# Gate and up projections of a SwiGLU layer as 2x2x2 block products with seven multiplications

## The chip, the cores and the metric

The kernel runs on one core of one Trainium2 chip. The metric is the device time of one execution in microseconds (us). The engines are named as in the profile: PE (TensorE, matmul), PEld (its weight loads), DVE (VectorE), ACT (ScalarE), POOL (GpSimd) and SP (SyncE, which here issues DMAs).

## The reference

One layer of a decoder, 512 tokens of 1024 channels, in float32: a mixer (stick-breaking attention and a gated convolution), a cross-attention to 256 memory tokens, and the feed-forward sublayer that the change is about, which ends in a final norm. Each has its own RMS norm and residual addition.

```python
hf = rms_norm(x, norm_ffn[l])
gate, up = jnp.split(hf @ w_ffn_in[l], 2, axis=-1)      # 1024 -> 2 x 2816
x = x + (jax.nn.silu(gate) * up) @ w_ffn_out[l]         # 2816 -> 1024
...
return rms_norm(x, norm_final)
```

## The kernel before

Activations lie transposed, features on the 128 partitions and the 512 tokens along the free axis. A matrix product is a loop over k tiles of 128 input features, and every product of two float32 values is made of three float32r matmuls: each operand is split into a high part (a cast on ACT, line 149 for weights, line 168 or 171 for activations) and a low part (a subtraction on DVE, line 150, 169 or 172), and `mm3` (lines 154 to 156) adds high x high, high x low and low x high into one PSUM bank.

`load_w` (line 138) loads 128 x 1024 weights over SP's queue into a `wr` buffer and splits them into `wh` and `wl`; each of the three has four buffers. `gemm` (line 158) runs eight k tiles, 24 matmuls of 512 columns, into one bank. The activations' parts come from `upool`, 50 buffers of 128 x 512, and float32 temporaries from `tpool`, seven.

`residual` (line 481) computes x + w.T @ act for eight feature tiles m, keeps the new x, splits x times the next norm's gain into two parts, and adds up the squares. The norm's factor 1/rms is not in these parts: it is applied to the results of the next product. `squares_mean` (line 176) gives it, along the tokens, by two matmuls of the squares' sum (`acch`, `accl`) into `varb` (line 196) and a short chain on ACT and DVE (lines 124 to 130); for this sublayer it is called `r2b`.

The gate and up projections (lines 578 to 593) loop over the 22 hidden tiles m of 128. For each, a `gemm` of the gate columns goes to tile `fg`, one of the up columns to `fu`; DVE scales both by `r2b` (lines 585 and 591), ACT applies Silu to the gate (line 586), DVE multiplies them (line 592), and the product is split into two parts. The matmuls for the token means stand between the first gate and the first up product.

Then the output projection runs over the hidden tiles k: each is 24 matmuls, three for each of eight output tiles, which occupy all eight PSUM banks. The last four k tiles are kept back (`HOLD`), and `finish` (line 613) runs them for one half of the tokens and then the other, 256 columns at a time: for each m it adds the residual (line 621), squares it on ACT (line 625) and adds up the squares on DVE (line 627). `store` (line 636) multiplies by the final norm's factor, on POOL for the first half and on DVE and POOL for the second (line 641), and writes the output.

The order on each engine is set at compile time by a scheduler that goes by the program's order and by what is ready; waits for data and for free buffers follow from the tiles.

Of the kernel before, what the change touches and what calls it, by code (L numbers as in the profile page):

```python
# [8 lines left out]
F32 = mybir.dt.float32  # L9
F32R = mybir.dt.float32r  # L10
# [14 lines left out]
HID = 2816  # L25
NF = HID // P
EPS = 1e-6
HOLD = 4                # FFN-out k tiles kept back, so that the last sum can finish by token half
MEM_AT = (1, 3, 5, 7)   # attention steps that square the memory's tiles
MEAN_AT = 9             # and the step that takes their mean, between two pairs of heads  # L30
EARLY = 2               # merge tiles whose gate projections run beside the attention
FIRST = 4               # weight loads that queue behind the stream's

# [4 lines left out]
def hybrid_layer(ctx: ExitStack, tc: tile.TileContext, xT_d, memT_d, cols_d, wv_d, win_d,  # L38
# [40 lines left out]

# [1 line left out]
    ident = cpool.tile([P, P], F32, tag="ident", name="ident")  # L81
# [29 lines left out]
    def log_exp_tables(last):  # L111
        """Has the table set that holds both Ln and Exp loaded behind an instruction."""
        i = nc.scalar.preload_act_table_set("natural_log_exp_and_others")
        after(i, [last])
        return [i]

    def rstd_of(var, n, s, tables=()):
        """1 / sqrt(var + eps) for [P, n] mean squares, refined by one Newton step."""
        def new(t):
            return tmp(t, n) if n > TT else spool.tile([P, n], F32, tag=t, name=nm(t))  # L120

        v, y, a = new("rv"), new("ry"), new("ra")
        r = cpool.tile([P, n], F32, tag=s, name=nm(s))
        after(nc.scalar.activation(y, var, AF.Ln, bias=eps_t), tables)
        nc.vector.tensor_scalar(out=v, in0=var, scalar1=EPS, scalar2=None, op0=ALU.add)  # L125
        exps.append(nc.scalar.activation(y, y, AF.Exp, scale=-0.5))
        nc.vector.tensor_tensor(out=a, in0=y, in1=y, op=ALU.mult)
        nc.vector.scalar_tensor_tensor(out=a, in0=a, scalar=-0.5, in1=v, op0=ALU.mult,
                                       op1=ALU.mult)
        nc.vector.scalar_tensor_tensor(out=r, in0=a, scalar=1.5, in1=y, op0=ALU.add, op1=ALU.mult)  # L130
        return r

    def chained(i):
        """Keeps the first loads in their order of issue."""
        after(i, chain[-1:])
        chain.append(i)

    def load_w(src, cols=P):
        """Loads [P, 1024] of weights and splits them into two float32r parts."""
        k = D // cols  # L140
        raw = wpool.tile([P, D], F32, tag="wr", name=nm("wr"))
        i = nc.sync.dma_start(raw, src)
        if count[1] < FIRST:
            count[1] += 1
            chained(i)
        hi = wpool.tile([P, k, cols], F32R, tag="wh", name=nm("wh"))
        lo = wpool.tile([P, k, cols], F32R, tag="wl", name=nm("wl"))
        h2, l2 = (t.rearrange("p k c -> p (k c)") for t in (hi, lo))
        nc.scalar.copy(h2, raw)  # L149
        nc.vector.tensor_tensor(out=l2, in0=raw, in1=f(h2), op=ALU.subtract)  # L150
        return hi, lo
# [6 lines left out]
    def gemm(ps, w, act, k0=0):  # L158
        """ps[feature, token] = sum over k of w[k].T @ act[k]."""
        n = len(act)  # L160
        for k in range(n):
            mm3(ps, (w[0][:, k0 + k, :], w[1][:, k0 + k, :]), act[k], k == 0, k == n - 1)

    def split(src, s, scale=None, cols=512):
        """src (* scale) as two float32r parts; src may lie in PSUM."""
        hi, lo = unit(s + "h", cols), unit(s + "l", cols)
        if scale is None:
            nc.scalar.copy(hi, src)
            nc.vector.tensor_tensor(out=lo, in0=src, in1=f(hi), op=ALU.subtract)
        else:  # L170
            nc.scalar.activation(hi, src, AF.Copy, scale=scale)
            nc.vector.scalar_tensor_tensor(out=lo, in0=src, scalar=scale, in1=f(hi),
                                           op0=ALU.mult, op1=ALU.subtract)
        return hi, lo

    def squares_mean(acc, n):
        """acc: the squares' sum over feature tiles, for n tiles of tokens."""
        parts = unit("acch", n * P), unit("accl", n * P)
# [3 lines left out]
        def by_token(s, tables=()):  # L182
            """1 / rms with tokens on partitions, [P, n]."""
            vp = otile("var")
# [7 lines left out]
        def along(s, tables=()):  # L192
            """1 / rms with tokens along the free axis, on all partitions."""
            vp = otile("varb")[:, :n * P]
# [5 lines left out]

# [1 line left out]
    xg, wv = [], []  # L202
# [16 lines left out]

# [1 line left out]
    vps = [ztile("v") for _ in range(TT)]  # L221
# [6 lines left out]

# [1 line left out]
    def project(col):  # L230
# [49 lines left out]

    # ---- stick-breaking attention, z^T by key tile and two heads; the weights that follow a key
    # tile's own are summed on the tensor engine, in the bank that holds z ----
    oT = []
# [91 lines left out]
    def mem_square(k2):  # L375
        """The squares' sum of two feature tiles of the memory."""
        mk = f(unit("mk")).rearrange("p (j t) -> p j t", j=2)
# [36 lines left out]
    stick.close()  # L414
    xpool = ctx.enter_context(tc.tile_pool(name="xpool", bufs=12))

# [1 line left out]
    mg = []  # L418
# [12 lines left out]

# [1 line left out]
    merged = []  # L433
# [18 lines left out]

# [1 line left out]
    km = []  # L454
# [25 lines left out]

    def residual(w_dram, act, old, gain):
        """x^T = old + w.T @ act; x^T, x^T * gain in two parts, and the squares' mean of x."""
        xs, xn = [], []
        acc = tmp("acc")
        for m in range(KD):
            w = load_w(w_dram[m])
            ps = mmtile("r")
            gemm(ps, w, act)
            xm = xpool.tile([P, S], F32, tag="x", name=nm("x"))
            if old is None:  # L490
                nc.sync.dma_start(xm, xT_d[m * P:(m + 1) * P, :])
            nc.vector.tensor_tensor(out=xm, in0=ps, in1=xm if old is None else old[m], op=ALU.add)
            xs.append(xm)
            xn.append(split(xm, "xg", gain[:, m:m + 1]))
            if m == 0:
# [8 lines left out]

# [1 line left out]
    om = []  # L506
# [66 lines left out]

    x2T, x2g, mean2 = residual(wmo_d, om, x1, g_ffn)

# [1 line left out]
    act = []  # L577
    for m in range(NF):
        w = load_w(wfi_d[m])
        ps = mmtile("fg")  # L580
        gemm(ps, w, x2g)
        if m == 0:
            r2b = mean2[1]("r0b")
        g = tmp("fg")
        nc.vector.tensor_tensor(out=g, in0=ps, in1=r2b, op=ALU.mult)  # L585
        silu = nc.scalar.activation(g, g, AF.Silu)
        w = load_w(wfi_d[NF + m])
        ps = mmtile("fu")
        gemm(ps, w, x2g)
        u = tmp("fu")  # L590
        nc.vector.tensor_tensor(out=u, in0=ps, in1=r2b, op=ALU.mult)  # L591
        nc.vector.tensor_tensor(out=u, in0=u, in1=g, op=ALU.mult)
        act.append(split(u, "act"))

# [1 line left out]
    acc = [mmtile("f") for _ in range(2)] + [ztile("f") for _ in range(4)]  # L596
    acc = acc[2:] + [otile("f") for _ in range(2)] + acc[:2]

    def out_step(m, k, w, sl):
        fs = slice(m * P, (m + 1) * P)  # L600
        mm3(acc[m][:, sl], (w[0][:, 0, fs], w[1][:, 0, fs]), (act[k][0][:, sl], act[k][1][:, sl]),
            k == 0, k == NF - 1, skip_group_check=True)

    for k in range(NF - HOLD):
        w = load_w(wfo_d[k], D)
        for m in range(KD):
            out_step(m, k, w, slice(0, S))
    held = [load_w(wfo_d[k], D) for k in range(NF - HOLD, NF)]
    tables = log_exp_tables(silu)
    hs = S // 2  # L610
    yg = {}

    def finish(half):
# [3 lines left out]
        for m in range(KD):  # L617
            for i, w in enumerate(held):
                out_step(m, NF - HOLD + i, w, sl)
            y = x2T[m][:, sl]  # L620
            nc.vector.tensor_tensor(out=y, in0=acc[m][:, sl], in1=y, op=ALU.add)
            if m == 0:
# [33 lines left out]
def _layout(x, mem, norm_mix, w_in, conv_w, w_branch_a, w_branch_b, w_mix_out, norm_mem_q,  # L656
# [3 lines left out]
    def by_column(w, cols=P, k=KD):  # L660
        """[K, N] -> [N / cols, P, K / P, cols], flat in each partition."""
        n = w.shape[1] // cols
        return w.reshape(k, P, n, cols).transpose(2, 1, 0, 3).reshape(n, P, k * cols)

    def by_row(w):
        """[1024, 512] -> [4, P, 2 * 512]."""
        return w.reshape(4, 2, P, 512).transpose(0, 2, 1, 3).reshape(4, P, 1024)

    gains = np.stack([norm_mix[0], norm_mem_q[0], norm_mem_kv[0], norm_ffn[0], norm_final])
# [14 lines left out]
        "w_mem_o": by_column(w_mem_o[0]),  # L684
        "w_ffn_in": by_column(w_ffn_in[0]),
        "w_ffn_out": w_ffn_out[0].reshape(NF, P, D),
# [19 lines left out]
```

## Time and profile before

| What | Value |
|---|---|
| Median of 3 runs | 900.91 us (899.91 to 901.19) |
| The profiled execution: span from first to last instruction | 901.2 us |
| PE busy, share of the span | 883.5 us, 98% |
| PEld busy | 735.6 us, 82% |
| DVE busy | 497.7 us, 55% |
| ACT busy | 370.4 us, 41% |
| POOL busy | 40.0 us, 4% |

The profile is of one execution; its span is that execution's time, 0.3 us above the median of the runs. A line such as "L155 PE MATMUL fu<-xgl,wh 128*128 128x512 f32 x176 | 68.5, 389 | 0.0" is a group of instructions: program line, engine, operation, output and inputs, shapes, count, then busy us, mean ns of one, and idle us of the engine before them. In a timeline, the two numbers ahead are start and length in us. Matmuls are pipelined, so their recorded lengths overlap.

### The profile page before, as it was taken

How to read it: one execution, taken by the hardware profiler on the slowest of the kernel's cores; microseconds unless marked ns; L12 is line 12 of the kernel's file. 1: busy time of each engine (PE TensorE's matmuls, PEld its weight loads, DVE VectorE, ACT ScalarE, POOL GpSimd, SP SyncE). 2: the span in 40 equal slices, each digit the busy share in tenths (PEclk: the TensorE clock that was granted, in tenths of full speed). 3: DMA queues.
4: the chain of work that ended last, by engine and by line, in shares of the span. 5: the costliest groups of instructions: out<-in, count | busy, mean ns of one | idle time of the engine just before them, and what ended most of it. 6: DMA issues, size and time to landing. Idle time of an engine off the chain costs nothing.

```text
span 901.2 us, 10745 instructions
## 1 busy us (share of the span) xinstructions
PE 883.5 (98%) x4210; PEld 735.6 (82%) x4210; DVE 497.7 (55%) x751; ACT 370.4 (41%) x607; POOL 40.0 (4%) x89
## 2 busy tenths in 40 slices
PE   7999999999999999999999999999999999999995
PEld 5878887888888898888888888888888888888894
DVE  5768787886544566555546564444444434322236
ACT  6566565565332344433434442222332223221133
POOL 0021221111000000000000000000000000000003
PEclk9999999999999999999999999999999999999998
DMA  7332212226222245432121222233222233222202
GB/s 280 117 106 82 82 60 70 71 71 211 94 94 93 94 140 188 145 111 96 48 71 46 95 94 94 96 100 107 95 94 94 94 97 109 98 94 93 71 1 94
DMA packets 29490, 89.85 MB, mean 100 GB/s; under 512 B 3056, under 2 KB 7168, under 8 KB 29440
## 3 DMA queue, kind: packets, MB, share of 16 engines
q1 hardware_dynamic: 28864, 88.62, 28.9%
q8 instruction: 33, 0.54, 0.3%
q10 hardware_dynamic: 544, 0.52, 0.2%
q14 instruction: 17, 0.14, 0.1%
q0 software_dynamic: 32, 0.03, 0.0%
HBM read 87.06 MB, written 2.10 MB: 99 GB/s over the span
## 4 chain that ended last, share of the span: by engine, by line
PE 96%; DVE 2%; ACT 1%; DMA 0%; issue 0%; DVEq 0%; POOL 0%; POOLq 0%; ACTq 0%
PE pr L154 7%; PE pr L155 7%; PE pr L156 7%; PE fu L155 4%; PE fg L155 4%; PE fg L156 4%; PE fu L156 4%; PE fu L154 4%; PE fg L154 4%; PE f L154 4%; PE f L155 4%; PE f L156 4%; PE r L154 3%; PE r L155 3%; PE r L156 3%; PE mq L154 2%
## 5 line engine op out<-in xcount | busy, mean ns | idle before, releaser
L149 ACT CAST wh<-wr 128x1024 fp32r<-128x1024 f32 x150 | 157.6, 1052 | 424.0 <-issue 175.6
L150 DVE TENSOR_TENSOR wl<-wr,wh 128x1024 fp32r<-128x1024 f32 x150 | 183.5, 1223 | 121.2 <-ACT wh L149 120.9
L154 PE MATMUL pr<-xgh,wh 128*128 128x512 f32 x288 | 113.0, 392 | 0.1
L156 PE MATMUL pr<-xgh,wl 128*128 128x512 f32 x288 | 112.5, 391 | 0.0
L155 PE MATMUL pr<-xgl,wh 128*128 128x512 f32 x288 | 112.5, 390 | 0.0
L154 PE MATMUL f<-acth,wh 128*128 128x512 f32 (+1 forms) x208 | 74.4, 358 | 0.0
L155 PE MATMUL f<-actl,wh 128*128 128x512 f32 (+1 forms) x208 | 74.0, 356 | 0.0
L156 PE MATMUL f<-acth,wl 128*128 128x512 f32 (+1 forms) x208 | 74.0, 357 | 0.0
L155 PE MATMUL fu<-xgl,wh 128*128 128x512 f32 x176 | 68.5, 389 | 0.0
L154 PE MATMUL fu<-xgh,wh 128*128 128x512 f32 x176 | 68.5, 389 | 0.0
L154 PE MATMUL fg<-xgh,wh 128*128 128x512 f32 x176 | 68.5, 389 | 0.0
L156 PE MATMUL fg<-xgh,wl 128*128 128x512 f32 x176 | 68.5, 389 | 0.0
L155 PE MATMUL fg<-xgl,wh 128*128 128x512 f32 x176 | 68.5, 389 | 0.0
L156 PE MATMUL fu<-xgh,wl 128*128 128x512 f32 x176 | 68.5, 389 | 0.0
L154 PEld LDWEIGHTS pr<-xgh,wh 128*128 128x128 f32 x288 | 54.4, 189 | 11.5 <-issue 0.4
L156 PEld LDWEIGHTS pr<-xgh,wl 128*128 128x128 f32 x288 | 54.2, 188 | 11.4
L155 PEld LDWEIGHTS pr<-xgl,wh 128*128 128x128 f32 x288 | 54.3, 188 | 10.8
L591 DVE TENSOR_TENSOR fu<-fu,r0b 128x512 f32<-128x512 f32 x22 | 15.2, 691 | 66.8 <-PE fu L156 66.8
L154 PEld LDWEIGHTS f<-acth,wh 128*128 128x128 f32 x208 | 39.3, 189 | 6.0 <-DVE rv L125 0.2
L155 PEld LDWEIGHTS f<-actl,wh 128*128 128x128 f32 x208 | 39.3, 189 | 5.6
L156 PEld LDWEIGHTS f<-acth,wl 128*128 128x128 f32 x208 | 39.1, 189 | 5.7
L585 DVE TENSOR_TENSOR fg<-fg,r0b 128x512 f32<-128x512 f32 x22 | 15.2, 692 | 49.0 <-PE fg L156 48.9
(216 smaller groups left out, 1655.2 us busy)
## 6 DMA issues: line engine op xcount, KB each, us to landing
wr<-in_w_ffn_in_dram SPq DMA_DIRECT2D x44, 512.0 KB, 3.2
wr<-in_w_in_dram SPq DMA_DIRECT2D x36, 512.0 KB, 3.3
wr<-in_w_ffn_out_dram SPq DMA_DIRECT2D x22, 512.0 KB, 3.2
wr<-in_w_branch_dram SPq DMA_DIRECT2D x8, 512.0 KB, 3.2
wr<-in_w_mem_k_dram SPq DMA_DIRECT2D x8, 512.0 KB, 3.3
wr<-in_w_mem_v_dram SPq DMA_DIRECT2D x8, 512.0 KB, 3.9
wr<-in_w_mix_out_dram SPq DMA_DIRECT2D x8, 512.0 KB, 3.3
wr<-in_w_mem_q_dram SPq DMA_DIRECT2D x8, 512.0 KB, 3.2
```

The costliest lines, as they stand in the source:

```text
L149: nc.scalar.copy(h2, raw)
L150: nc.vector.tensor_tensor(out=l2, in0=raw, in1=f(h2), op=ALU.subtract)
L154: nc.tensor.matmul(ps, a[0], b[0], start=start, stop=False, **kw)
L155: nc.tensor.matmul(ps, a[0], b[1], start=False, stop=False, **kw)
L156: nc.tensor.matmul(ps, a[1], b[0], start=False, stop=stop, **kw)
L585: nc.vector.tensor_tensor(out=g, in0=ps, in1=r2b, op=ALU.mult)
L591: nc.vector.tensor_tensor(out=u, in0=ps, in1=r2b, op=ALU.mult)
```

## The change

The 1024 input features are taken as four pairs of k tiles, the tokens as two halves of 256, and a hidden tile's gate and up columns as the two output rows: a 2x2 block matrix of weights times a 2x2 block matrix of activations. Seven products of blocks (Strassen's scheme in Winograd's form) take the place of eight. For each hidden tile m:

- `ffn_weights` loads gate and up weights (two loads of 128 x 1024, in a new layout in which the two k tiles of each pair are apart) and forms four sums of 128 x 512: s1, s2 and s4 on POOL, each from the one before, and s3 on DVE. The two gate blocks are split in one piece of 1024 columns, the other five operands (s1, s2, s3, s4 and one up block) in pieces of 512.
- `product` runs one block product: four pairs x three split terms, 12 matmuls of 256 columns.
- `ffn_pair` strings the seven products together. Some add to a bank that holds an earlier product; ACT copies the sum so far out of PSUM first (c1, u2, u3), and DVE adds what belongs together. PE's order is written out: the products 4, 5, 6 of tile m alternate with 1, 2, 3 of tile m + 1, then comes 7 of tile m. The token means' matmuls stand behind the first three products.
- Only the gate is scaled by `r2b`; the up side's factor is applied behind the output projection, in `finish`, by a multiplication out of PSUM ahead of the residual's addition.
- The residual before this stage makes, for each pair of feature tiles, the seven activation forms (`forms_of`: four additions on DVE, seven casts on ACT, seven subtractions on DVE, all 256 wide). They hold 28 of the 50 `upool` buffers, the unsplit activations 22; the activations are split behind the loop.
- `x` is updated in place, with `xpool` at 8 buffers for 12, and comments are taken out.

```diff
+    def forms_of(xe, xo):
+        b12, b22 = xe[:, HS:], xo[:, HS:]
+        c = tmp("c1")
+        n1, t3 = c[:, :HS], c[:, HS:]
+        nc.vector.tensor_tensor(out=n1, in0=xe[:, :HS], in1=b12, op=ALU.subtract)
+        nc.vector.tensor_tensor(out=t3, in0=b22, in1=b12, op=ALU.subtract)
+        c = tmp("c2")
+        n2, t4 = c[:, :HS], c[:, HS:]
+        nc.vector.scalar_tensor_tensor(out=n2, in0=n1, scalar=-1.0, in1=b22, op0=ALU.mult,
+                                       op1=ALU.subtract)
+        nc.vector.scalar_tensor_tensor(out=t4, in0=n2, scalar=-1.0, in1=xo[:, :HS], op0=ALU.mult,
+                                       op1=ALU.subtract)
+        made = []
+        for raw in (xe[:, :HS], xo[:, :HS], n1, n2, t3, t4, b22):
+            u = unit("xf")
+            nc.scalar.copy(u[:, :HS], raw)
+            nc.vector.tensor_tensor(out=u[:, HS:], in0=raw, in1=f(u[:, :HS]), op=ALU.subtract)
+            made.append(u)
+        return made
...
-            xn.append(split(xm, "xg", gain[:, m:m + 1]))
+            if pairs:
+                raw = tmp("xr")
+                nc.scalar.activation(raw, xm, AF.Copy, scale=gain[:, m:m + 1])
+                if m % 2:
+                    xn.append(forms_of(even, raw))
+                else:
+                    even = raw
+            else:
+                xn.append(split(xm, "xg", gain[:, m:m + 1]))
...
-    for m in range(NF):
-        w = load_w(wfi_d[m])
-        ps = mmtile("fg")
-        gemm(ps, w, x2g)
-        if m == 0:
-            r2b = mean2[1]("r0b")
+    KP = KD // 2
+    def parts(raw, pool, tag):
+        w = pool.tile([P, 2, 512], F32R, tag=tag, name=nm("wf"))
+        nc.scalar.copy(w[:, 0, :], raw)
+        nc.vector.tensor_tensor(out=w[:, 1, :], in0=raw, in1=f(w[:, 0, :]), op=ALU.subtract)
+        return w[:, 0, :], w[:, 1, :]
+    def ffn_weights(m):
+        wg = wpool.tile([P, D], F32, tag="wr", name=nm("wr"))
+        nc.sync.dma_start(wg, wfi_d[m][:, :D])
+        wu = wpool.tile([P, D], F32, tag="wr", name=nm("wr"))
+        nc.sync.dma_start(wu, wfi_d[m][:, D:])
+        a21, a22 = wu[:, :512], wu[:, 512:]
+        s1 = fpool.tile([P, 512], F32, tag="w2", name=nm("s1"), bufs=4)
+        nc.gpsimd.tensor_tensor(out=s1, in0=a21, in1=a22, op=ALU.add)
+        s3 = fpool.tile([P, 512], F32, tag="w2", name=nm("s3"), bufs=4)
+        nc.vector.tensor_tensor(out=s3, in0=wg[:, :512], in1=a21, op=ALU.add)
+        hi = wpool.tile([P, D], F32R, tag="wh", name=nm("wh"))
+        lo = wpool.tile([P, D], F32R, tag="wl", name=nm("wl"))
+        nc.scalar.copy(hi, wg)
+        nc.vector.tensor_tensor(out=lo, in0=wg, in1=f(hi), op=ALU.subtract)
+        a11, a12 = wg[:, :512], wg[:, 512:]
+        s2 = fpool.tile([P, 512], F32, tag="w2", name=nm("s2"), bufs=4)
+        nc.gpsimd.tensor_tensor(out=s2, in0=s1, in1=a11, op=ALU.add)
+        s4 = fpool.tile([P, 512], F32, tag="w2", name=nm("s4"), bufs=4)
+        nc.gpsimd.tensor_tensor(out=s4, in0=s2, in1=a12, op=ALU.add)
+        return [(hi[:, :512], lo[:, :512]), (hi[:, 512:], lo[:, 512:]), parts(s1, wpool, "wh"),
+                parts(s2, wpool, "wl"), parts(s3, wpool, "wh"), parts(a22, wpool, "wl"),
+                parts(s4, fpool, "wf")]
+    def product(ps, w, i, first, last):
+        ps = ps[:, :HS]
+        for k in range(KP):
+            hi, lo = (x[:, k * P:(k + 1) * P] for x in w[i])
+            x = x2f[k][i]
+            for j, (a, b) in enumerate(((lo, x[:, :HS]), (hi, x[:, :HS]), (hi, x[:, HS:]))):
+                nc.tensor.matmul(ps, a, b, start=first and k == 0 and j == 0,
+                                 stop=k == KP - 1 and j == 2, skip_group_check=True)
+    def ffn_pair(m):
+        w = ffn_weights(m)
+        z, v, y = ztile("z"), ztile("v"), otile("y")
+        sa, sb = tmp("sa"), tmp("sb")
+        c1, u2, u3, c22 = sa[:, :HS], sa[:, HS:], sb[:, :HS], sb[:, HS:]
         g = tmp("fg")
...
+        product(z, w, 0, True, True)
+        nc.scalar.copy(c1, z[:, :HS])
+        yield
+        product(v, w, 1, True, True)
+        nc.vector.tensor_tensor(out=g[:, :HS], in0=v[:, :HS], in1=c1, op=ALU.add)
+        yield
+        product(y, w, 2, True, True)
+        yield
+        product(z, w, 3, False, True)
+        nc.scalar.copy(u2, z[:, :HS])
+        yield
+        product(z, w, 4, False, True)
+        nc.scalar.copy(u3, z[:, :HS])
+        nc.vector.tensor_tensor(out=c22, in0=y[:, :HS], in1=u3, op=ALU.add)
+        yield
+        product(z, w, 5, False, True)
+        yield
+        product(y, w, 6, False, True)
+        nc.vector.tensor_tensor(out=g[:, HS:], in0=y[:, :HS], in1=u2, op=ALU.add)
+        nc.vector.tensor_tensor(out=g, in0=g, in1=r2b[0], op=ALU.mult)
+        silu[0] = nc.scalar.activation(g, g, AF.Silu)
+        a = f(unit("act"))
+        for half, u in enumerate((z[:, :HS], c22)):
+            sl = slice(half * HS, (half + 1) * HS)
+            nc.vector.scalar_tensor_tensor(out=a[:, sl], in0=u, scalar=-1.0, in1=g[:, sl],
+                                           op0=ALU.mult, op1=ALU.mult)
+        act.append(a)
+        yield
+    silu, r2b = [None], [None]
+    with tc.manual_schedule(engines={mybir.EngineType.PE}):
+        now = ffn_pair(0)
+        for _ in range(3):
+            next(now)
+        r2b[0] = mean2[1]("r0b")
+        for m in range(NF):
+            then = ffn_pair(m + 1) if m + 1 < NF else iter(())
+            for _ in range(3):
+                next(now)
+                next(then, None)
+            next(now)
+            now = then
...
+    act = [split(a, "act") for a in act]
...
-            nc.vector.tensor_tensor(out=y, in0=acc[m][:, sl], in1=y, op=ALU.add)
+            up = tmp("up", hs)
+            nc.vector.tensor_tensor(out=up, in0=acc[m][:, sl], in1=r2b[:, sl], op=ALU.mult)
+            nc.vector.tensor_tensor(out=y, in0=up, in1=y, op=ALU.add)
```

More of the change, by code (lines that the diff above doesn't have):

```diff
@@ L26 @@
 NF = HID // P
+HS = S // 2
 EPS = 1e-6
@@ L414, in hybrid_layer @@
     stick.close()
-    xpool = ctx.enter_context(tc.tile_pool(name="xpool", bufs=12))
+    xpool = ctx.enter_context(tc.tile_pool(name="xpool", bufs=8))
+    fpool = ctx.enter_context(tc.tile_pool(name="fpool", bufs=2))
     mg = []
@@ L479, in hybrid_layer, with residual @@
             vm[t][n] = split(pss[t], "vm", rm[:, t:t + 1])
-    def residual(w_dram, act, old, gain):
+    def forms_of(xe, xo):
[17 more added lines that the diff above has]
+        return made
+    def residual(w_dram, act, old, gain, pairs=False):
         xs, xn = [], []
@@ L488, in residual @@
             gemm(ps, w, act)
-            xm = xpool.tile([P, S], F32, tag="x", name=nm("x"))
             if old is None:
+                xm = xpool.tile([P, S], F32, tag="x", name=nm("x"))
                 nc.sync.dma_start(xm, xT_d[m * P:(m + 1) * P, :])
-            nc.vector.tensor_tensor(out=xm, in0=ps, in1=xm if old is None else old[m], op=ALU.add)
+            else:
+                xm = old[m]
+            nc.vector.tensor_tensor(out=xm, in0=ps, in1=xm, op=ALU.add)
             xs.append(xm)
-            xn.append(split(xm, "xg", gain[:, m:m + 1]))
+            if pairs:
[5 more added lines that the diff above has]
+                    even = raw
+            else:
+                xn.append(split(xm, "xg", gain[:, m:m + 1]))
             if m == 0:
@@ L572, in hybrid_layer @@
             om.append(split(ps, "om"))
-    x2T, x2g, mean2 = residual(wmo_d, om, x1, g_ffn)
+    x2T, x2f, mean2 = residual(wmo_d, om, x1, g_ffn, True)
     act = []
-    for m in range(NF):
-        w = load_w(wfi_d[m])
-        ps = mmtile("fg")
-        gemm(ps, w, x2g)
-        if m == 0:
-            r2b = mean2[1]("r0b")
-        g = tmp("fg")
[L585 to L593, printed above, removed]
+    KP = KD // 2
@@ L596, in hybrid_layer @@
+    silu, r2b = [None], [None]
[11 more added lines that the diff above has]
+            now = then
+    silu, r2b = silu[0], r2b[0]
     acc = [mmtile("f") for _ in range(2)] + [ztile("f") for _ in range(4)]
@@ L609, in hybrid_layer @@
     tables = log_exp_tables(silu)
-    hs = S // 2
+    hs = HS
     yg = {}
@@ L667, in by_row, with by_pair @@
         return w.reshape(4, 2, P, 512).transpose(0, 2, 1, 3).reshape(4, P, 1024)
+    def by_pair(w):
+        return w.reshape(KD // 2, 2, P, 2, NF, P).transpose(4, 2, 3, 1, 0, 5).reshape(NF, P, 2048)
     gains = np.stack([norm_mix[0], norm_mem_q[0], norm_mem_kv[0], norm_ffn[0], norm_final])
@@ L684, in _layout @@
         "w_mem_o": by_column(w_mem_o[0]),
-        "w_ffn_in": by_column(w_ffn_in[0]),
+        "w_ffn_in": by_pair(w_ffn_in[0]),
         "w_ffn_out": w_ffn_out[0].reshape(NF, P, D),
```

## The prediction

> **What bounds the kernel now.** I read the page first: busy shares, then the chain that ended last, then the groups of the gate and up projections.
>
> ```profile
> span 901.2 us, 10745 instructions
> PE 883.5 (98%) x4210; PEld 735.6 (82%) x4210; DVE 497.7 (55%) x751; ACT 370.4 (41%) x607; POOL 40.0 (4%) x89
> PE 96%; DVE 2%; ACT 1%; DMA 0%; issue 0%; DVEq 0%; POOL 0%; POOLq 0%; ACTq 0%
> L155 PE MATMUL fu<-xgl,wh 128*128 128x512 f32 x176 | 68.5, 389 | 0.0
> ```
>
> PE is busy 98% of the span and carries 96% of the chain, so whatever shortens PE's stream shortens the kernel, as long as nothing else becomes late. The 389 ns of one matmul is not its price: matmuls overlap in the records. The price is the distance between starts, and for that I took the windows by stage and the timeline of PE. In the windows, the columns after the stretch are its length, then busy us and instruction count of PE, PEld, DVE, ACT and POOL, then clock, DMA share and GB/s.
>
> ```profile
> 323.20:346.30 23.10, 23.09 (x192) 22.89 (x191) 17.50 (x27) 12.01 (x18) 0.00 (x0) 1.00 0.49 160
> 526.90:766.80 239.90, 239.90 (x1059) 198.57 (x1058) 114.16 (x138) 75.67 (x93) 0.00 (x0) 1.00 0.29 97
> ```
>
> ```profile
> 526.92 0.39 PE L154 MATMUL fg<-xgh,wh 128*128 128x512 f32 x1
> ...
> 766.80 0.39 PE L154 MATMUL f<-acth,wh 128*128 128x512 f32 x1
> ...
> 869.07 0.28 PE L156 MATMUL f<-acth,wl 128*128 128x256 f32 x1
> ...
> 876.27 0.28 PE L156 MATMUL f<-acth,wl 128*128 128x256 f32 x1
> ```
>
> The stage to be changed runs from 526.92 to 766.80: 239.9 us for 22 hidden tiles x 48 matmuls of 512 columns, plus two for the token means, 1058 in all. That is 0.2267 us each, without a gap, at clock 1.00. Matmuls of 256 columns exist in two other stages: 60 steps from 869.07 to 876.27 are 0.1200 us each, and the memory keys' 192 fill 23.10 us, 0.1203 us each. So half the columns cost 53% and not 50%.
>
> **PE's part of the change.** Seven products replace eight. Each is 4 pairs of k tiles x 3 split terms = 12 matmuls of 256 columns; 22 x 7 x 12 = 1848. At 0.1200 us they take 221.8 us, with the two means 222.2 us, against 239.9: **-17.7 us**. An eighth off the 239.4 us of 1056 matmuls would be 29.9; 12.2 of that goes to the poorer price of the short matmul. The Trainium skill (TensorE: Matmul & The Clock Gate, Back-to-back issue gap) gives a warm matmul of 256 columns 256/2.4 + 2.5 = 109 ns, by which an estimate of the stage is some 20 us less still; two stages of this trace show 120, so the trace decides.
>
> One hidden tile (gate and up) thus gets 84 x 0.120 = 10.08 us of PE, where it had 10.88. What the other engines must do in it grows:
>
> ```profile
> L150 DVE TENSOR_TENSOR wl<-wr,wh 128x1024 fp32r<-128x1024 f32 x150 | 183.5, 1223 | 121.2 <-ACT wh L149 120.9
> L585 DVE TENSOR_TENSOR fg<-fg,r0b 128x512 f32<-128x512 f32 x22 | 15.2, 692 | 49.0 <-PE fg L156 48.9
> L169 DVE TENSOR_TENSOR actl<-fu,acth 128x512 fp32r<-128x512 f32 x22 | 14.9, 685 | 1.8 <-ACT acth L168 1.8
> L621 DVE TENSOR_TENSOR x<-f,x 128x256 f32<-128x256 f32 x16 | 6.7, 421 | 1.6 <-PE f L156 1.1
> L149 ACT CAST wh<-wr 128x1024 fp32r<-128x1024 f32 x150 | 157.6, 1052 | 424.0 <-issue 175.6 <-PE f L155 76.4 <-PE fg L155 70.4
> L168 ACT CAST acth<-fu 128x512 fp32r<-128x512 f32 x22 | 13.5, 623 | 12.7 <-DVE fu L592 12.7
> L345 ACT ACTIVATE a<-z 128x256 f32<-128x256 f32 x16 | 6.1, 381 | 1.0 <-DVE al L349 1.0
> ```
>
> ACT: one 1024-wide cast, five 512-wide, three copies out of PSUM, one Silu: 1.05 + 5 x 0.62 + 3 x 0.38 + 0.62 = 5.9 us, 59% of the 10.08. It does not bind. DVE before: two 1024-wide and four 512-wide, 5.2 us. DVE after: one 1024-wide (1.22), seven 512-wide (s3, five low parts, the scaling by r2b; 7 x 0.69 = 4.8), five 256-wide (5 x 0.42 = 2.1): 8.1 us by recorded length. Independent neighbours overlap at their ends:
>
> ```profile
> 500.83 1.22 DVE L150 TENSOR_TENSOR wl<-wr,wh 128x1024 fp32r<-128x1024 f32 x1 [0.21 <-ACT wh L149]
> 501.97 0.74 DVE L172 SCALAR_TENSOR_TENSOR xgl<-x,gcol,xgh 128x512 fp32r<-128x512 f32 x1
> ```
>
> The second starts 1.14 after the first, 0.08 before its end, so thirteen operations take 8.1 - 13 x 0.08 = 7.1, say 7.2 us. DVE alone is at 71 to 81%. Its new neighbour is POOL, idle in this stage before (0.00 in the window), which gets three 512-wide additions per tile. Where both run, in the last 20 us, the trace shows this:
>
> ```profile
> 881.00 5.42 POOL L641 TENSOR_TENSOR yg<-yg,rf 128x512 f32<-128x512 f32 x4 [668.29 <-PE f L156]
> ```
>
> ```profile
> 882.23 0.42 DVE L621 TENSOR_TENSOR x<-f,x 128x256 f32<-128x256 f32 x1 [0.37 <-PE f L156]
> 882.65 2.62 DVE L627 TENSOR_TENSOR sq<-sq,sq 128x256 f32<-128x256 f32 x2
> 885.19 0.41 DVE L621 TENSOR_TENSOR x<-f,x 128x256 f32<-128x256 f32 x1
> 886.08 0.62 DVE L627 TENSOR_TENSOR sq<-sq,sq 128x256 f32<-128x256 f32 x1 [0.49 <-ACT sq L625]
> 887.52 0.42 DVE L627 TENSOR_TENSOR sq<-sq,sq 128x256 f32<-128x256 f32 x1 [0.48 <-ACT sq L625]
> ```
>
> From 881.00 to 886.42 POOL does four 512-wide multiplications. L621, with one input in PSUM, keeps its 0.42 us beside them. L627, both inputs in SBUF, needs 0.42 alone (887.52) but two took 2.62 and one 0.62 beside POOL. So a DVE operation with two SBUF inputs and a POOL operation take turns, and one turn of POOL costs DVE (2.62 - 0.84)/2 = 0.9 to 1.0 us. POOL's price per operation lies between that and (5.42 - 2 x 0.42)/4 = 1.15, the group's length without DVE's two turns. By the Trainium skill (SBUF — State Buffer, Who interferes with whom) the second to issue "**fully blocks** until the first finishes"; by that rule, the trace agrees.
>
> Of DVE's 7.2 us only four 256-wide operations read PSUM (4 x 0.34 = 1.4 us) and can run beside POOL. Per tile, DVE and POOL together need between 7.2 + 3 x 0.95 - 1.4 = 8.7 (all four hidden, no turn lost) and 8.1 + 3 x 1.15 = 11.6 us (full records, nothing hidden). PE's 10.08 lies between, so this is the term that decides. From the turn cost and spacing, 7.2 + 2.9 = 10.1 before overlap; DVE also waits, in order, behind ACT's casts (in the row at 500.83 for 0.21 us), so I add 0.2: **10.3 us per tile, 0.22 x 22 = +4.8 us** over PE's own pace (0 to +33).
>
> The other waits of the loop are covered. Where sums go on in one bank, at least one product of another bank, 1.44 us, lies between, for the copy of what is there so far. That copy needs about 0.42 (matmul start to reader, next part) + 0.38 - 0.12 = 0.7 us. Weight parts are made up to a tile ahead; their buffers come free three or more products (4.3 us) before they are needed. Bytes are the same: 97 GB/s becomes about 105, and the key stage above ran at 160.
>
> **Edges.** The forms of the earlier pairs cost nothing: per feature tile of the residual DVE has 0.69 + 1.22 + 0.69 + half of 11 x 0.34 = 4.5 us beside 5.4 of PE. Only the last pair is bare, on the way into the stage:
>
> ```profile
> 526.70 0.39 PE L156 MATMUL r<-omh,wl 128*128 128x512 f32 x1
> ...
> 532.37 0.39 PE L196 MATMUL varb<-acch,mean_r 128*128 128x512 f32 x1
> ```
>
> ```profile
> 527.12 0.69 DVE L492 TENSOR_TENSOR x<-r,x 128x512 f32<-128x512 f32 x1 [2.05 <-PE r L156]
> ...
> 531.01 0.69 DVE L180 TENSOR_TENSOR accl<-acc,acch 128x512 fp32r<-128x512 f32 x1
> ```
>
> The squares' sum is ready at 531.70, and PE wants it at 532.37, after 24 matmuls. In the new order it wants it after three products, 36 x 0.120 = 4.3 us, at 531.2: 0.5 late at once. In front of it on DVE now also stand that pair's forms, 4 + 7 operations of 256 (3.7 us). PE's order is fixed, so it stands: 0.5 if the forms go behind, 4.2 if they go in front, and up to 8 with a backlog from the first tile's weight sums. I take **+4**.
>
> Out of the stage: the last tile has no successor to interleave, so two copies lie bare, 2 x 0.7 = 1.4; and the third output bank is the one of the last product sums, free after 0.42 + 0.42 + 0.69 + 0.62 + 0.42 = 2.6 us behind the last product, with two tiles (6 x 0.227 = 1.4 us) in front: 1.2. **+2.5** (0.5, if the two output tiles are swapped and the copies quick, to 5). The 22 splits moved behind the loop find buffers only when the last tile's products let go of their forms (28 forms and 22 activations fill the 50 of `upool`), but the first output tile needs only the first of them, and each takes 0.69 us of DVE against 24 x 0.227 = 5.4 us of PE per k tile: hidden.
>
> The tail:
>
> ```profile
> 889.11 0.42 DVE L621 TENSOR_TENSOR x<-f,x 128x256 f32<-128x256 f32 x1
> 889.11 0.28 PE L156 MATMUL f<-acth,wl 128*128 128x256 f32 x1
> 890.41 0.42 DVE L621 TENSOR_TENSOR x<-f,x 128x256 f32<-128x256 f32 x1
> ```
>
> Here DVE, not PE, ends last, one feature tile per 1.30 us. A scaling of 0.42 is added to each, in front of an addition that now has both inputs in SBUF: 1.7 us a tile against PE's 12 x 0.12 = 1.44. The lag grows 0.26 a tile instead of shrinking by 0.15, over five tiles 2.1, plus 0.4 on the last: **+2.5** (0.5, if the scaling fits into DVE's wait for the squares, to 6, if three more turns of POOL fall in).
>
> **Sum.** 901.2 - 17.7 + 4.8 + 4 + 2.5 + 2.5 = 897.3 us in the profiled execution. Its span lies 0.3 above the median of the runs, 900.91, so I forecast **897.0**.
>
> **Rivals.** (1) DVE and POOL become the bound. This is the same turn-taking, but with recorded lengths, not spacings, as DVE's cost: 8.1 + 2.9 + 0.2 = 11.2 us per tile is 1.1 x 22 = 24.6 over PE's pace and gives 901.2 - 17.7 + 24.6 + 9 = 917; break-even is at 10.08 + 8.7/22 = 10.47 us per tile. For it: one loses the gain with 0.2 us a tile more than I take, and all operations but four compete. Against it: DVE that lags never waits for ACT, and idle DVE time lets POOL through. The skill's rule above is the mechanism of this case. (2) The turns fall into idle DVE time and the edges cost their lower ends: 901.2 - 17.7 + 0.5 + 0.5 + 0.5 = 885. For it: DVE has 10.08 - 7.2 = 2.9 us free in each tile, about POOL's three turns. Against it: the turns come where the low parts are made, not where DVE rests. (3) The gain is eaten by the edges and a period near 10.47, and nothing is seen: 899 to 903.
>
> **Numbers.** This measurement tells 0.2% (1.8 us) from no change. My forecast 0.46 (its own range 888 to 899), rival 1 beyond 0.2% 0.30, rival 2 0.12, rival 3 0.12. Faster: 0.46 + 0.12 = 0.58; same 0.12; slower 0.30. The range 886 to 914 leaves out about 0.05 below (the best of rival 2) and 0.14 above (the worse half of rival 1).
>
> **What would show it.** In the profile after: 1848 products 0.120 us apart inside a tile; a window over the loop of about 227 us; DVE low parts of 512 columns with a mean well over 0.69 us, POOL additions over 1.15; PE waiting at the token means for accl. If PE's idle time in the loop is put down to DVE's low parts and exceeds 9 us, rival 1 holds and I am wrong. If the products are not 0.120 apart with their operands ready, the first term is wrong.

## The result: 2.8% slower, and the profile after

The changed kernel takes 926.12 us (median of 4 runs, 924.28 to 928.22), the kernel before 900.78 (899.91 to 901.19): a ratio of 1.0282 [1.0262 to 1.0302]. The forecast, 897.0 with a range up to 914, was wrong.

From the page of the kernel after: span, busy shares, chain, and the group with the most idle time of PE.

```profile
span 925.4 us, 12937 instructions
PE 875.8 (95%) x5002; PEld 763.1 (82%) x5002; DVE 639.9 (69%) x979; ACT 441.2 (48%) x789; POOL 135.2 (15%) x155
PE 78%; DVE 15%; ACT 3%; issue 2%; DMA 1%; DVEq 0%; POOL 0%; ACTq 0%; SPq 0%; POOLq 0%
L654 PE MATMUL z<-xf,wf 128*128 128x256 f32 x792 | 109.0, 288 | 21.4 <-ACT sa L673 20.6
```

PE is less busy than before (875.8 for 883.5 us), as intended, but its share of the chain fell from 96 to 78% and DVE's rose from 2 to 15%. 20.6 us of PE's idle time are put down to one line of ACT: L673, the 256-wide copy of u2.

The timeline of the kernel after, PE's rows at three of these waits, and the window of one steady tile (columns as in the prediction's windows):

```profile
549.39 1.69 PE L654 MATMUL z<-xf,wf 128*128 128x256 f32 x12 [0.97 <-ACT sa L673]
560.66 1.58 PE L654 MATMUL z<-xf,wf 128*128 128x256 f32 x11 [0.97 <-ACT sa L673]
...
755.32 0.86 PE L654 MATMUL z<-xf,wf 128*128 128x256 f32 x5 [0.97 <-ACT sa L673]
```

```profile
541.40:552.70 11.30, 10.33 (x86) 10.13 (x86) 10.23 (x14) 6.80 (x12) 4.42 (x3) 1.00 0.23 75
```

A tile takes 560.66 - 549.39 = 11.27 us instead of 84 x 0.120 = 10.08. The stall is 1.2 us by the distance of starts (0.97 in the records, whose ends overlap). Counting the hidden tiles from 0, it comes in 18 of the 19 tiles 1 to 19, always at product 5; two of the 18 waits are much longer (1.74 and 2.39 us). Why the copy is late shows in the same timeline around one wait:

```profile
646.89 1.59 PE L654 MATMUL z<-xf,wf 128*128 128x256 f32 x12
648.32 0.28 PE L654 MATMUL z<-xf,wl 128*128 128x256 f32 x1
649.52 0.40 PE L654 MATMUL z<-xf,wh 128*128 128x256 f32 x2
650.89 1.34 PE L654 MATMUL z<-xf,wf 128*128 128x256 f32 x9 [0.97 <-ACT sa L673]
...
647.86 0.41 DVE L682 TENSOR_TENSOR fg<-y,sa 128x256 f32<-128x256 f32 x1
648.31 1.61 DVE L683 TENSOR_TENSOR fg<-fg,r0b 128x512 f32<-128x512 f32 x1
...
649.95 0.63 ACT L684 ACTIVATE fg<-fg 128x512 f32<-128x512 f32 x1 [2.19 <-DVE fg L683]
650.49 0.35 ACT L673 COPY sa<-z 128x256 f32<-128x256 f32 x1
...
648.07 1.29 POOL L640 TENSOR_TENSOR s<-s,wr 128x512 f32<-128x512 f32 x1 [1.29 <-issue]
```

Read it from the bottom. POOL's s2 addition (L640) starts at 648.07. DVE's scaling of the gate (L683, both inputs in SBUF) issues at 648.31 and takes 1.61 us, where 0.69 is its price alone. Silu (L684) of the same tile m waits for it, and ACT with it: 2.19 us idle. Behind Silu in ACT's order stands the copy of u2 of tile m + 1 (L673), though the product that it copies, started at 646.89, had ended about 648.3. Product 5 needs the bank that is copied. In between PE has one product, from 648.32 to about 649.8, 1.44 us, and then waits until 650.89. The turn of POOL itself costs about 0.9 us on DVE; it reaches PE because ACT's order stands between. One tile of the loop shows it by itself: in tile 12 POOL's s2 addition starts just behind the scaling and not ahead of it (670.94 and 670.86), the scaling takes 0.69 us, and product 5 has no wait.

Only DVE operations with both inputs in SBUF are longer, as the DVE groups of the kernel after show between 530 and 800 us:

```profile
L683 DVE TENSOR_TENSOR fg<-fg,r0b 128x512 f32<-128x512 f32 x22 | 31.7, 1440 | 0.8
L633 DVE TENSOR_TENSOR s<-wr,wr 128x512 f32<-128x512 f32 x20 | 29.7, 1487 | 3.6 <-DMA wr<-in_w_ffn_in_dram 2.0
L688 DVE SCALAR_TENSOR_TENSOR act<-sb,fg 128x256 f32<-128x256 f32 x22 | 25.7, 1167 | 0.0
L688 DVE SCALAR_TENSOR_TENSOR act<-z,fg 128x256 f32<-128x256 f32 x22 | 9.3, 424 | 2.5 <-ACT fg L684 0.7
```

The last two are the same instruction: 1167 ns with `sb` from SBUF, 424 with `z` from PSUM. This bears out the rule of the Trainium skill that the prediction drew on (SBUF — State Buffer, Who interferes with whom; the words that it quotes stand in that page's Summary: rules for kernel authors), here for additions.

The edges of the stage, PE's and ACT's rows in the timeline of the kernel after:

```profile
524.01 0.28 PE L654 MATMUL z<-xf,wl 128*128 128x256 f32 x1
...
526.99 0.39 PE L654 MATMUL v<-xf,wl 128*128 128x256 f32 x1 [0.31 <-ACT xf L500]
...
529.03 0.39 PE L654 MATMUL v<-xf,wh 128*128 128x256 f32 x1 [1.54 <-DVE xf L501]
...
532.40 0.47 PE L197 MATMUL varb<-acch,mean_r 128*128 128x512 f32 x1 [1.56 <-DVE acch L180]
533.51 0.50 PE L197 MATMUL varb<-accl,mean_r 128*128 128x512 f32 x1 [0.65 <-DVE accl L181]
...
778.99 1.58 PE L654 MATMUL y<-xf,wf 128*128 128x256 f32 x12
784.41 0.79 PE L155 MATMUL f<-acth,wh 128*128 128x512 f32 x1 [3.83 <-ACT acth L169]
...
781.80 0.63 ACT L684 ACTIVATE fg<-fg 128x512 f32<-128x512 f32 x1 [3.44 <-DVE fg L683]
782.45 1.28 ACT L114 ACT_TABLE_LOAD   x1
783.74 2.71 ACT L169 CAST acth<-act 128x512 fp32r<-128x512 f32 x5
```

On the way in, PE waits four times: twice for the last pair's forms, twice for the squares' sum. Three products and two means would take 524.01 + 36 x 0.120 + 2 x 0.227 = 528.8; the loop goes on at 533.85, 5.1 us late. On the way out, the last product ends about 780.4, but the first output matmul starts at 784.41: the splits stand behind the last Silu and behind the table load of 1.28 us. Behind these waits, on both sides of the stage, PE runs at a lower granted clock for some us, as two windows show:

```profile
533.85:538.20 4.35, 4.35 (x25) 4.35 (x24) 4.24 (x6) 2.21 (x4) 3.23 (x2) 0.61 0.00 0
784.41:790.80 6.39, 6.39 (x15) 4.75 (x16) 6.39 (x11) 6.20 (x12) 0.00 (x0) 0.51 0.00 0
```

By the distance of starts, 24 matmuls of 256 columns take 4.36 us (533.85 to 538.21) instead of 2.88, and 14 of 512 take 6.38 (784.41 to 790.79) instead of 3.17: 1.5 and 3.2 us more.

### The profile page after: what moved, and what is told of

Same layout as the page of the kernel before. It is cut to its first block, busy times and chain, and to the rows that moved or that the text cites. A ratio compares the mean times of both kernels' runs of the same rounds, so it can differ in the third digit from the quotient of the medians.

```text
span 925.4 us, 12937 instructions
## 1 busy us (share of the span) xinstructions
PE 875.8 (95%) x5002; PEld 763.1 (82%) x5002; DVE 639.9 (69%) x979; ACT 441.2 (48%) x789; POOL 135.2 (15%) x155
## 4 chain that ended last, share of the span: by engine, by line
PE 78%; DVE 15%; ACT 3%; issue 2%; DMA 1%; DVEq 0%; POOL 0%; ACTq 0%; SPq 0%; POOLq 0%
PE z L654 7%; PE pr L155 7%; PE pr L156 7%; PE pr L157 7%; PE f L155 4%; PE f L156 4%; PE f L157 4%; DVE wf L620 4%; DVE fg L683 3%; DVE s L633 3%; PE v L654 3%; PE r L156 3%; PE r L157 3%; PE r L155 3%; PE mq L157 2%
## 5 line engine op out<-in xcount | busy, mean ns | idle before, releaser
L150 ACT CAST wh<-wr 128x1024 fp32r<-128x1024 f32 x106 | 111.3, 1052 | 250.3 <-issue 85.9
L151 DVE TENSOR_TENSOR wl<-wr,wh 128x1024 fp32r<-128x1024 f32 x106 | 130.3, 1229 | 110.1 <-ACT wh L150 108.1
L654 PE MATMUL z<-xf,wf 128*128 128x256 f32 x792 | 109.0, 288 | 21.4 <-ACT sa L673 20.6
L654 PEld LDWEIGHTS z<-xf,wf 128*128 128x128 f32 x792 | 100.5, 193 | 25.7 <-ACT sa L673 24.7
L631 POOL TENSOR_TENSOR s<-wr 128x512 f32<-128x512 f32 x22 | 35.5, 1615 | 386.4 <-DMA wr<-in_w_ffn_in_dram 335.3
L619 ACT CAST wf<-s 128x512 fp32r<-128x512 f32 x88 | 54.3, 621 | 60.4 <-PE y L654 33.0
L654 PE MATMUL y<-xf,wf 128*128 128x256 f32 x528 | 66.7, 282 | 0.0
L620 DVE TENSOR_TENSOR wf<-s,wf 128x512 fp32r<-128x512 f32 x88 | 65.2, 743 | 2.2 <-ACT wf L619 0.9
L654 PEld LDWEIGHTS y<-xf,wf 128*128 128x128 f32 x528 | 64.6, 190 | 0.0
L684 ACT ACTIVATE fg<-fg 128x512 f32<-128x512 f32 x22 | 13.9, 630 | 46.5 <-DVE fg L683 46.5
```

What stands on the lines that cost most here:

```text
L619: nc.scalar.copy(w[:, 0, :], raw)
L620: nc.vector.tensor_tensor(out=w[:, 1, :], in0=raw, in1=f(w[:, 0, :]), op=ALU.subtract)
L631: nc.gpsimd.tensor_tensor(out=s1, in0=a21, in1=a22, op=ALU.add)
L654: nc.tensor.matmul(ps, a, b, start=first and k == 0 and j == 0, stop=k == KP - 1 and j == 2, skip_group_check=True)
L684: silu[0] = nc.scalar.activation(g, g, AF.Silu)
```

## The experiments

Theory Q, the queue: PE waits for u2 because the copy stands behind Silu in ACT's order. Theory C, capacity (the prediction's first rival): DVE and POOL together need more than PE's 10.08 us per tile, and any order would show it. A third part, the edges, adds to both. The ratios are to the kernel before, run alongside each.

**1. Silu behind the next u2 copy.** The generator gives way ahead of Silu, and Silu is held behind the copy. The two multiplications on DVE that need Silu's result stand behind it in the program and move with it:

```diff
-        nc.scalar.copy(u2, z[:, :HS])
+        held_copy.append(nc.scalar.copy(u2, z[:, :HS]))
...
+        yield
         silu[0] = nc.scalar.activation(g, g, AF.Silu)
+        after(silu[0], held_copy[-1:])
...
```

> Only ACT's order changes: the Silu of a hidden tile is queued behind the next tile's copy of u2, not ahead of it; POOL still makes three sums. Theory Q (a queue: POOL's turn delays DVE's scaling, the Silu waits for it, and the u2 copy behind the Silu holds PE 1.0 us per tile): the wait on u2 goes, the tile period falls from 11.28 to 10.1-10.4 us, the kernel from 926 to 902-908. Theory C (capacity: DVE with POOL's turns is itself the bound, busy 10.3 of 11.3 us per tile): another wait takes the place of this one, period 10.9 or more, kernel above 917.

Measured 914.70 us, 1.0159 [1.0144 to 1.0174]. The waits at L673 in the steady loop are gone, those at the next copy (u3, L676) have come. ACT's rows around one, and DVE's group:

```profile
593.08 0.63 ACT L685 ACTIVATE fg<-fg 128x512 f32<-128x512 f32 x1 [3.08 <-DVE fg L683]
...
594.39 0.37 ACT L676 COPY sb<-z 128x256 f32<-128x256 f32 x1
```

```profile
L683 DVE TENSOR_TENSOR fg<-fg,r0b 128x512 f32<-128x512 f32 x22 | 31.7, 1442 | 0.8
```

Silu still waits 3.08 us for DVE, and now it is u3's copy that stands behind it; PE's waits there are 0.27 to 0.91 us in most tiles that have one. 11.4 us came back. It does not decide between Q and C: the order moved the wait, which Q allows, but a tile still took 10.6 to 11.2 us, which C foretells.

**2. The three sums on DVE**, with **3. both edits together**:

```diff
-        nc.gpsimd.tensor_tensor(out=s1, in0=a21, in1=a22, op=ALU.add)
+        nc.vector.tensor_tensor(out=s1, in0=a21, in1=a22, op=ALU.add)
...
-        nc.gpsimd.tensor_tensor(out=s2, in0=s1, in1=a11, op=ALU.add)
+        nc.vector.tensor_tensor(out=s2, in0=s1, in1=a11, op=ALU.add)
...
-        nc.gpsimd.tensor_tensor(out=s4, in0=s2, in1=a12, op=ALU.add)
+        nc.vector.tensor_tensor(out=s4, in0=s2, in1=a12, op=ALU.add)
```

> All four weight sums on DVE, POOL idle in the loop; ACT's order as in the changed kernel. DVE loses POOL's turns (3 x about 0.9 us) and gains three 512-wide additions (3 x 0.61). Theory Q: the scaling takes 0.69 in place of 1.61 us, so the Silu comes 0.9 us earlier and PE's wait shrinks from 1.0 to 0.1-0.2 us: period 10.2-10.4, kernel 903-910. Theory C: DVE's need falls from 10.3 to about 9.2 us, below PE's 10.08: also 10.1-10.3. If moving three sums to DVE makes it slower than 926, turn-taking is not what costs.

> Silu behind the u2 copy and all sums on DVE. Both theories: nothing is left in front of PE in the loop, period 10.08-10.15, kernel 900-904: what is then left above the forecast's 883.5 at PE's own pace are the edges (into the loop, out of it, the tail).

Measured 898.90, 0.9976 [0.9966 to 0.9987], and 898.94, 0.9978 [0.9968 to 0.9989]. Of the kernel with the sums on DVE, the scaling's group and the window of 10.08 us, one tile:

```profile
L683 DVE TENSOR_TENSOR fg<-fg,r0b 128x512 f32<-128x512 f32 x22 | 15.1, 687 | 0.1
```

```profile
560.00:570.08 10.08, 10.08 (x86) 10.08 (x86) 9.14 (x17) 5.60 (x10) 0.00 (x0) 1.00 0.30 106
```

DVE does three more additions per tile and still has room: busy 9.14 of 10.08 us, and PE has no gap. Both kernels are a little faster than was expected of them; in the loop no wait is left. Having the three sums on POOL and not on DVE costs 27 us; with no turns taken, the order of Silu is worth nothing.

**4. Silu behind the next u3 copy**, the sums on POOL as in the change. Now no copy that PE waits for stands behind Silu (the rest is as in experiment 1, with the hold on u3's copy in place of u2's):

```diff
-        nc.scalar.copy(u3, z[:, :HS])
+        held_copy.append(nc.scalar.copy(u3, z[:, :HS]))
...
+            for i in range(3):
                 next(now)
+                if i == 1:
+                    next(last, None)
```

> POOL makes three sums, and the Silu is queued one product later than in a1, behind the next tile's copy of u3, so that no copy that PE waits for stands behind it. Theory Q (only the queue on ACT holds PE): period 10.1-10.2, kernel 900-904. Theory C (DVE and POOL together need about 10.5 us or more): the period stays at a1's 10.6-10.8, now by waits for weights, kernel 909-915.

Measured 901.12, 1.0004 [0.9986 to 1.0022]: 25 us better than the change, from the order of Silu and the two multiplications behind it. Two of its DVE groups (the scaling, and the multiplication with `sb` from SBUF), a window of one tile, and DVE's and ACT's rows in it:

```profile
L683 DVE TENSOR_TENSOR fg<-fg,r0b 128x512 f32<-128x512 f32 x22 | 30.8, 1401 | 0.7
L690 DVE SCALAR_TENSOR_TENSOR act<-sb,fg 128x256 f32<-128x256 f32 x22 | 10.4, 473 | 0.0
```

```profile
640.00:650.08 10.08, 10.08 (x87) 10.08 (x86) 9.25 (x14) 5.52 (x11) 4.62 (x4) 1.00 0.32 106
```

```profile
646.34 1.61 DVE L683 TENSOR_TENSOR fg<-fg,r0b 128x512 f32<-128x512 f32 x1
...
646.41 0.37 ACT L673 COPY sa<-z 128x256 f32<-128x256 f32 x1 [0.76 <-PE z L654]
...
649.62 0.64 ACT L685 ACTIVATE fg<-fg 128x512 f32<-128x512 f32 x1
```

POOL makes its three sums as before and the scaling takes 1.61 us as before, but the copy now waits for PE alone, Silu starts 1.7 us after the scaling's end, and PE shows no wait from the means to the last tile. One thing besides ACT's order changed: the multiplications come later on DVE, and s4's turn no longer falls on the one with two SBUF inputs (473 ns for 1167). So DVE has one turn less to pay for here, but the order alone did that, and C said that any order would show the loss. This refutes C: DVE, busy 9.25 of 10.08 us, has enough time beside POOL. The loss of the loop was the queue.

**5. One sum moved.** Only s2 goes to DVE, s1 and s4 stay on POOL:

```diff
-        nc.gpsimd.tensor_tensor(out=s2, in0=s1, in1=a11, op=ALU.add)
+        nc.vector.tensor_tensor(out=s2, in0=s1, in1=a11, op=ALU.add)
```

> Two sums on POOL (s1, s4), s2 and s3 on DVE; Silu as in the changed kernel. In the changed kernel it is s2's turn that falls on DVE's scaling. Theory Q: the scaling is free again unless another turn falls there; if none does, PE's wait is under 0.3 us and the kernel 900-908. Theory C alone: DVE's need falls by one turn less one addition (0.9 - 0.6 = 0.3 us per tile), kernel 917-921.

Measured 900.69, 1.0007 [0.9994 to 1.0021]. The same 25 us as experiment 4: of the three turns, the one that meets the scaling was what the loop paid for. With it gone L683 has a mean of 687 ns, while POOL's turns fall on other operations, the low part of the up block most of all (680 ns in the changed kernel):

```profile
L683 DVE TENSOR_TENSOR fg<-fg,r0b 128x512 f32<-128x512 f32 x22 | 15.1, 687 | 0.1
L620 DVE TENSOR_TENSOR wf<-wr,wf 128x512 fp32r<-128x512 f32 x21 | 35.5, 1688 | 0.0
```

In a window of one tile (600.00 to 610.08) DVE is busy 9.88 of 10.08 us, more than in experiment 4, and PE has no gap: a turn costs the loop nothing on an operation that no copy for PE stands behind. Moving s1 or s4 alone was not tried.

**6. The edges**, on the change (a4) and on the sums on DVE (b1). The means' matmuls come two products later, three splits stand ahead of the last tile's Silu, and the table load behind the last split:

```diff
-        r2b[0] = mean2[1]("r0b")
...
                 next(then, None)
+                if r2b[0] is None:
+                    r2b[0] = mean2[1]("r0b")
+            if m == NF - 1:
+                early = [split(a, "act") for a in act[:3]]
...
-    tables = log_exp_tables(silu)
+    tables = log_exp_tables(cast[-1])
```

> Only the edges: the token means' matmuls two products later, three of the activations' splits ahead of the last tile's end, the Ln/Exp tables loaded behind the last split. The loop is as in the changed kernel (period 11.28). Theory E (PE's waits of 2.2 us at the means and 3.8 us before the output projection each also cost the clock: some 1.5 and 2.8 us of matmuls at half rate behind them): kernel 8 to 11 us faster, 915-918, and no matmuls 0.43 us apart behind the loop. Rival (the waits only move, since DVE lags there): 0 to 4 us faster.

> All sums on DVE, and the two edges as in a4. If edges and loop are separate terms, a2's 898.9 falls by what the edges gave alone, 10.5 us: 886-891, about 1.3% faster than the kernel before. If the waits of one only hide those of the other: 895 or more.

Measured 915.66, 1.0166 [1.0149 to 1.0183], and 890.89, 0.9885 [0.9865 to 0.9906]: 10.5 us off the change, 8.0 off the kernel with the sums on DVE. PE's rows of the latter, at the means and at the end of the loop:

```profile
535.07 0.39 PE L197 MATMUL varb<-acch,mean_r 128*128 128x512 f32 x1
535.30 0.40 PE L197 MATMUL varb<-accl,mean_r 128*128 128x512 f32 x1
...
750.07 1.58 PE L654 MATMUL y<-xf,wf 128*128 128x256 f32 x12
751.50 0.40 PE L156 MATMUL f<-actl,wh 128*128 128x512 f32 x1
```

The means wait for nothing, the output follows the last product after 1.43 us, that product's own length, and the clock stays at 1.00 around both places.

**7. Without the up side's factor**, on the kernel with the sums on DVE and the edges mended (b1):

```diff
-            nc.vector.tensor_tensor(out=up, in0=acc[m][:, sl], in1=r2b[:, sl], op=ALU.mult)
-            nc.vector.tensor_tensor(out=y, in0=up, in1=y, op=ALU.add)
+            nc.vector.tensor_tensor(out=y, in0=acc[m][:, sl], in1=y, op=ALU.add)
```

> As b1, but the multiplication of the output projection's sums by the token factor (16 of 256 columns, ahead of the residual's addition) is left out, so the up side is not scaled. It measures the tail's price. By the trace, from the first short matmul to the end is 36.5 us in the kernel before and 39.9 in the changed one: 3 to 3.5 us below b1. If the longer tail came from elsewhere (POOL's turns against additions that read SBUF twice stay the same only if the factor is the cause): less than 1 us.

Measured 886.99, 0.9842 [0.9822 to 0.9863]: the factor costs 3.9 us by the medians, 3.4 by the two profiled executions (from the first short output matmul to the end 39.85 us with it, 36.44 without).

**8. The last pair last.** On the same kernel, products 1 to 3 of the first tile run their first three pairs before any of them needs the last:

```diff
+        if m == 0:
+            for i, ps in enumerate((z, v, y)):
+                product(ps, w, i, True, True, range(KP - 1))
+        left = range(KP - 1, KP) if m == 0 else range(KP)
...
```

> As b1, and the first tile's first three products run their three early pairs of k tiles first and the last pair, whose forms come latest, at the end. PE's two waits for those forms (0.3 and 1.5 us in the changed kernel) are then covered by 3.2 us of matmuls: 1 to 2 us faster than b1's 890.9, 888.5-890. Rival (DVE is behind there with the weights' sums, so the forms come late all the same): within 0.7 us of b1.

Measured 888.12, 0.9853 [0.9830 to 0.9877]: it beats both kernels, 1.5% faster than before. Its page:

```profile
span 886.8 us, 12843 instructions
PE 865.2 (98%) x5002; PEld 757.6 (85%) x5002; DVE 614.3 (69%) x1045; ACT 442.8 (50%) x789; POOL 40.2 (5%) x89
PE 95%; DVE 3%; ACT 1%; DMA 0%; issue 0%; DVEq 0%; POOL 0%; ACTq 0%; POOLq 0%
```

Its 2.8 us over b1 can't be put down to the edit: the two intervals overlap, they were not run side by side, and from the first product to the first mean the trace gives 524.74 to 533.09 here and 526.38 to 535.07 there, only 0.34 us less. The rest is a stage that began earlier.

## Why the prediction was wrong

**The step that failed** is "The other waits of the loop are covered". It priced the copy of u2 at 0.7 us and gave it one product, 1.44 us, of cover. Both numbers were right: without the turn that one sum takes, the loop has almost no wait (experiment 5). But the copy was priced as if ACT were free. The step did not ask what stands ahead of it in ACT's order: Silu of the tile before, which waits for a DVE operation that POOL can make 0.9 us longer. From 533.85 to the last tile's wait at 774.98, 148 products of 1.44 us would take 213.1 us and took 241.1; without the 1.5 of lower clock at its start and the 0.7 of that last wait, 26 us are the queue's. They are more than 18 x 1.2: in the tiles of the two longest waits DVE also stood waiting for weights (0.66 and 1.36 us at L633), and behind the wait of 1.74 the clock fell, for 1.6 us more. In experiment 4, with the queue mended, PE has none of these waits.

**The terms, one by one.** PE: right. The matmuls are 0.120 us apart (648.32 to 649.52 is ten steps), and 10.08 us a tile is what PE needs in experiments 2, 3 and 4; the -17.7 us were there. The turn of POOL: right in size (1.61 for 0.69 us). The term made of it, +4.8 us because DVE and POOL need 10.3 us a tile: wrong in size. Experiment 4 shows them keeping 10.08, so it is about 0, while the queue cost 26.

The edge into the stage, +4: undersized. It was 5.1 of waits, within the bounds, and 1.5 of lower clock, which no term held. The edge out, +2.5: the two bare copies were about as told (0.74 and 0.80 in the records, 0.9 and 1.0 by starts), but "the first output tile needs only the first of them" left out that even the first split stands behind the last Silu and a table load. That was 4.0 us of waiting and 3.2 of lower clock; with the copies about 8.7. Experiment 6 gives 10.5 us for what it mended of both edges. The tail, +2.5: 3.4 to 3.9 by experiment 7. Its working was wrong all the same, since DVE's lag does not grow by 0.26 a tile: in the timeline of the kernel after, the last three tiles' additions are 1.30 us apart, as before.

```profile
911.55 0.42 DVE L737 TENSOR_TENSOR x<-up,x 128x256 f32<-128x256 f32 x1
...
912.85 0.42 DVE L737 TENSOR_TENSOR x<-up,x 128x256 f32<-128x256 f32 x1
...
914.15 0.42 DVE L737 TENSOR_TENSOR x<-up,x 128x256 f32<-128x256 f32 x1
```

**Sum.** -17.7 + 26 + 6.6 + 8.7 + 3.9 = +27, against 24.2 between the two spans. The first product starts 2.9 us earlier than the first matmul of the stage did before (524.01 for 526.92). That makes the sum fit, but stages that the edits leave alone end at places that vary by this much between kernels here (526.38 and 524.74 above), and what makes them vary stays open.

**Rivals.** The first gave 917 and a test: PE's idle time put down to DVE's low parts, over 9 us. The idle time came, 20.6 us, put down to ACT's copy; the time was slower as this rival said, its mechanism was refuted by experiment 4. The second rival's 885 is near what the mended kernel reaches (888), but by coincidence: that kernel has no sums on POOL, and so no turns to fall into idle time.

## What to carry to other kernels

For each short operation that the busiest engine waits for, list what stands ahead of it in its own engine's queue and what that in turn waits for: a turn of 0.9 us, harmless in DVE's sum of busy time, cost about 1.2 us of PE or more in 18 of the 22 tiles. Work given to POOL is not free just because POOL is idle; look which DVE operations with two SBUF inputs it will meet, and whether an order-bound queue hangs on one of them. Where a stage is replaced, list what must be done between its last product and the next stage's first, and add the slower matmuls after the gap to its price.

## What the hardware showed that was not expected

Waits of a few us can cost PE more than their own length. After 0.31, 1.54, 1.56 and 0.65 us of waiting within 6.8 us, the granted clock was 0.61 over the next 4.35 us; after one of 3.83 us it was 0.51 over the next 6.39 us. Most tiles of the steady loop, with 0.97 us of waiting in each, left it at 1.00. The Trainium skill (TensorE: Matmul & The Clock Gate, Part 1) has the clock halve after an idle window of about 3.4 us; the single wait of 3.83 agrees with it. Of the waits on the way in none is that long, and the clock fell all the same. Nor does length alone decide within the loop, as PE's rows at its two longest waits show (the first row holds 8 of the product's 12 matmuls):

```profile
684.58 1.83 PE L654 MATMUL z<-xf,wf 128*128 128x256 f32 x8 [1.74 <-ACT sa L673]
687.06 0.41 PE L654 MATMUL v<-xf,wl 128*128 128x256 f32 x1
...
744.04 1.69 PE L654 MATMUL z<-xf,wf 128*128 128x256 f32 x12 [2.39 <-ACT sa L673]
745.57 0.28 PE L654 MATMUL v<-xf,wl 128*128 128x256 f32 x1
```

After the wait of 1.74 us the product of 12 matmuls takes 2.48 us from its start to the next product's (a granted clock of 0.56 from 684.58 to 687.30); after the longer one of 2.39 us it takes 1.53. Whether waits add up within one window or something else decides, no run here tells apart.
